# A decoder layer with routed experts: routing tile by tile, small fills of the output, first weights ahead of the lists, another first pair

## The chip, the cores and the metric

The kernel runs on one core of one Trainium2 chip. The metric is the device time of one execution in microseconds: the median over the runs, 5215.67 us for the kernel before (three runs, 5214.3 to 5219.2).

## The reference

2048 tokens of 1024 channels pass through one layer in float32:

```python
# token mix: three branches from one input projection, merged by sigmoid gates
z = h @ w_in                                  # conv B,C,h | gMLP u,v | attention q | gates
y_conv = cb * causal_depthwise_conv(cc * ch, conv_w)
y_gmlp = gmlp_spatial_gate(gelu(gu), gelu(gv), ...)
y_xa   = memory_cross_attention(q, mem_n, w_kv)
merged = g_conv*(y_conv@w_conv_proj) + g_gmlp*(y_gmlp@w_gmlp_proj) + g_xa*(y_xa@w_xa_proj)
x = layer_norm(ALPHA * x + merged @ w_out)
# experts: top 4 of 32, gate = softmax of the four logits
logits = x @ w_router + b_router
top_vals, top_idx = top_k(logits, 4)
g, u = split(xs @ w_gate_up[e] + b_gate_up[e], 2)       # xs: the tokens of expert e
act  = (clip(u, -7, 7) + 1) * (min(g, 7) * sigmoid(1.702 * min(g, 7)))
y[token] += gate * (act @ w_down[e] + b_down[e])
x = layer_norm(ALPHA * x + y)
```

## The kernel before

All large products run on TensorE as three passes of the fp32r type: each operand is split into a high part (ScalarE, line 75) and a low part (VectorE, line 76), and hi x hi, lo x hi and hi x lo are added in PSUM. A weight unit is 1 MB, [128 x 8 x 256]; SyncE loads it into a raw buffer (`load_unit`), the two engines split it by halves into a ring (`whi`, `wlo`). `run_items` walks one list of items (a weight source, a TensorE function, an epilogue): before each item it issues splits and loads some halves ahead. Work without weights stands as items with no source, or as functions in the list `bg`, of which one is taken per item. The engines run in the order in which this walk writes their instructions.

*Token mix.* Four chunks of 512 tokens. In chunk 1 sixteen items without weights (`fill`, line 807) write the last layer norm's bias over the output, 128 rows each, since final results are later added to it. In the last chunk the order is: projection unit 2 of the third branch (weights `vd`), output-weight units 0 and 1, projection unit 3, output-weight units 2 and 3, then four token tiles in which `last_pe` (line 1473) multiplies the merged gates with the output weights (PSUM `lo`), and `last_epi` (line 1499) adds the residual `r` and does the layer norm. `x1_tr` transposes the result for the router (`lg`). `route_tasks` (line 606) chooses the experts, places tokens in the `lists` by scatters on GpSimd, and forms the gates' transpose (`gT`) that starts the sum `yacc`. The first two tiles are routed together after the last `lo`, then the third and the fourth each.

*Experts.* `rank` (line 707) sorts the experts by load; each rank has a fixed capacity (`CAPS`: 552, 532, 476, 460, ... 260 for ranks 0, 1, 2, 3, 15; 216 down to 52 for ranks 16 to 31), and `number` reads the expert's id (`eid`) on SyncE. `ORDER` makes pairs of a light and a heavy rank; the first pair is the lightest and rank 15, and rank 2 is last. An expert has eight up units (g0, u0, ... u3) and four down units. SyncE loads its list (`lst`), GpSimd gathers tokens (`xg`), TensorE transposes them (`xsT`), the split gives `xs`. A heavy expert's ups have weights stationary and all tokens as columns (`up`), a light one's have tokens stationary (`tu`, token-major) and its activations are transposed (`acT`); downs are `dn`, scatter-added into `yacc`. The ups of one expert run between the downs of the one before. `bulk` (line 984) computes the last layer norm while the last expert's downs (`ld`, line 850) run, and `again` (line 1085) redoes the rows that the last expert changed.

The order of the first pair's parts, and the start before it:

```python
l, h, nxt = exps[:3]
l.number()
h.number()
def start(_):
    for x in (l, h):
        x.list()
...
(l,"g",0),(l,"u",0),(l,"g",1),(l,"u",1),(h,"g",0),(h,"u",0),(l,"g",2),(l,"u",2),
(h,"g",1),(h,"u",1),(l,"g",3),(l,"u",3), ...
```

Of the kernel before, what the change touches and what calls it, by code (L numbers as in the profile page):

```python
# [51 lines left out]


LAST = 2
FIRST = HALF - 1
# [6 lines left out]
class Kern:  # L62
    def __init__(self, ctx, tc, a, out, dbg=None):
        self.ctx, self.tc, self.nc, self.a, self.out, self.dbg = ctx, tc, tc.nc, a, out, dbg or {}
        self.items = []
        self.bg = []

        self.qt = []
        self.post = []
        self.scat = None  # L70
        self.loaded = False

# [33 lines left out]
    def item(self, src, pe, epi=None, split=None):  # L106
        self.items.append((src, pe, epi, split or self.split_half))


    def run_items(self, first=None):  # L110
# [7 lines left out]
        def load(upto):  # L118
            nonlocal nl
            while nl < min(upto, len(wi)):  # L120
                raws[wi[nl]] = self.load_unit(items[wi[nl]][0])
                nl += 1

# [15 lines left out]
        for i in range(n):  # L139
            if items[i][0] is not None:  # L140
                done += 1

                split(2 * done + self.whalves - 3)
                load(ns // 2 + self.wraws)
                split(2 * done + max(2, self.whalves - 2))
# [5 lines left out]
            if self.bg:  # L151
                self.bg.pop(0)()
            if items[i][2] is not None:
# [117 lines left out]
    def phase_a(self):  # L271
# [12 lines left out]
        with ExitStack() as c2:  # L284
# [3 lines left out]
            self.pm = c2.enter_context(tc.tile_pool(name="pm", bufs=1))  # L288
            self.pp = c2.enter_context(tc.tile_pool(name="pp", bufs=3, space=PSUM))
# [4 lines left out]
            self.bst = pa.tile([3 * NE, D], F32R, name="bst")  # L294
            self.gtt = pa.tile([3 * NE, TC], F32R, name="gtt")
# [18 lines left out]
            for c in chunks:  # L314
                c.emit(chunks[c.c + 1] if c.c + 1 < NCHUNK else None)
            self.run_items()
            while self.bg:
# [229 lines left out]
    def router(self, t, th, tl):  # L547
        nc = self.nc
        te, ve = nc.tensor, nc.vector
        ps = self.tr_psum("lg")  # L550
        for k in range(KT):
# [3 lines left out]
        sm = self.sm  # L555
# [50 lines left out]
    def route_tasks(self, c, ts, tag=("t4", 2)):  # L606
# [6 lines left out]
        def choose():  # L613
# [5 lines left out]
            scr = self.pa.tile([P, 2, TC], F32, tag=tag[0], name="rscr", bufs=tag[1])  # L619
            if n == 1:  # L620

                scr, S["scr"] = (scr[:, i, :].rearrange("p (a b) -> p a b", a=2) for i in range(2))
# [13 lines left out]
        def place():  # L636
# [5 lines left out]
            scr = S["scr"] if n == 1 else self.pa.tile([P, 2, TC], F32, tag="t4", name="rscr2", bufs=2)  # L642
# [14 lines left out]
            ent = sm.tile([P, n, TOPK, 2], I32, tag="ent", name="ent", bufs=2)  # L657
# [13 lines left out]

            for t in range(n):
# [9 lines left out]
        def spread():  # L682
            gs = S["gs"]
            pt = self.tr_psum("gT")
            for t in range(n):
                te.transpose(pt[: 3 * NE, t * P : t * P + P], gs[:, t].rearrange("p h e -> p (h e)"), self.ident)
            se.activation(self.gtt[:, t0 * P : (t0 + n) * P], pt[: 3 * NE, : n * P], AF.Copy)

        return [choose, place, spread]


    def yacc_init(self, c, t, r, hs=range(2)):
        nc = self.nc
        row = c * TC + t * P
        for q in hs:
# [4 lines left out]
            if c < NCHUNK - 1:  # L700
                nc.sync.dma_start(self.yacc[q][row : row + P, :], x)
        if c == NCHUNK - 1:
            for h in range(2):
                nc.scalar.dma_start(self.yacc[h][row : row + P, :], r[:, t, h * 512 : h * 512 + 512])
# [34 lines left out]
    def moe(self, c3):  # L739
# [5 lines left out]
        self.wp2 = c3.enter_context(tc.tile_pool(name="wp2", bufs=1))  # L745
        self.whalves, self.nhalf = 6, 0
# [4 lines left out]
    def experts(self):  # L751
# [4 lines left out]
        h.number()  # L756

        def start(_):
            for x in (l, h):
                x.list()  # L760
# [7 lines left out]
        def prep(t):  # L768
# [5 lines left out]
            (l, "g", 0), (l, "u", 0), (l, "g", 1), (l, "u", 1), (h, "g", 0), (h, "u", 0), (l, "g", 2), (l, "u", 2),  # L774
# [31 lines left out]
    def fill(self, t):  # L806
        self.nc.gpsimd.dma_start(self.out[t * P : t * P + P, :], self.a["ln2_b"][0].partition_broadcast(P))
# [133 lines left out]
    def block(self, i):  # L941
# [10 lines left out]
        y = self.px.tile([P, D], F32, tag="xsb", name="yg")  # L952
# [4 lines left out]
    def eitem(self, e, kind, j, todo=()):  # L957
# [19 lines left out]
        self.item((e, kind, j), pe, epi)  # L977
# [6 lines left out]
    def bulk(self):  # L984
# [4 lines left out]
        def load(i):  # L989
            for t in (2 * i, 2 * i + 1):  # L990
                y = S["y"][t % 6]
# [3 lines left out]
        def start():  # L995
# [5 lines left out]
            self.acc = [px.tile([P, D], F32, tag="xg", name="xa", bufs=2) for _ in range(2)] + [w[:, 1, :], S["y"][4]]  # L1001

            self.res = [px.tile([P, D], F32, tag="yrb", name="res"), S["y"][5]]
# [5 lines left out]
        def mean(i):  # L1009
            y1 = S["y"][(2 * i + 1) % 6]  # L1010
# [9 lines left out]
        def stats(i):  # L1020
            y0, y1 = (S["y"][t % 6] for t in (2 * i, 2 * i + 1))
# [27 lines left out]
        def apply(i):  # L1049
            rs, nmr = S.pop(i)  # L1050
            for n, t in enumerate((2 * i, 2 * i + 1)):
                y = S["y"][t % 6]
                se.activation(y, y, AF.Identity, scale=rs[:, n : n + 1], bias=nmr[:, n : n + 1])
                ve.tensor_tensor(y, y, self.g2, ALU.mult)  # L1054
            for t in (2 * i, 2 * i + 1):
                gp.dma_start(self.out[t * P : t * P + P, :], S["y"][t % 6], accum_op=ALU.add)  # L1056
# [11 lines left out]
        def second(i):  # L1068
# [25 lines left out]
    def redo(self, e, t, x, y):  # L1094
        gp, ve, sm = self.nc.gpsimd, self.nc.vector, self.sm
        m = e.rows(t)
        if e.r is None:
            self.bb2 = self.px.tile([P, D], F32, tag="X", name="bb2")
            self.bcast_row(self.bb2, self.a["ln2_b"][0])
            self.g2 = self.px.tile([P, D], F32, tag="acta", name="g2")  # L1100
# [15 lines left out]
class Chunk:  # L1116
# [12 lines left out]
    def emit(self, nxt):  # L1129
# [164 lines left out]
    def proj_item(self, b, w, src, j):  # L1294
# [4 lines left out]
        k.item(w[:, j * UC : j * UC + UC], pe, self.proj_epi(b, j))  # L1299

    def projections(self, b, w, src, js):
        for j in js:
            for i, item in enumerate((lambda: self.gate_item(b, j), lambda: self.proj_item(b, w, src, j))):
                item()
                if self.c == 1 and b < 2:
                    self.k.item(None, lambda _, t=(b * NU + j) * 2 + i: self.k.fill(t))
# [120 lines left out]
    def out_epi(self, j):  # L1427
        k, ve = self.k, self.k.nc.vector

        def epi(ps):  # L1430
            r = self.r[:, :, j * UC : j * UC + UC]
            ve.scalar_tensor_tensor(r, r, ALPHA, ps, ALU.mult, ALU.add)
            if j == NU - 1:
# [11 lines left out]
                choose, place, spread = k.route_tasks(self.c, range(TT))  # L1445
                k.bg += [lambda: (k.router_top(), choose()), lambda: None, place, spread]
# [26 lines left out]
    def last_pe(self, t):  # L1473
        k, te = self.k, self.k.nc.tensor

        def pe(_):
# [3 lines left out]
            for q in range(2):  # L1480
                for j in range(NU):

                    if t >= 2 and (q, j) == (0, 1):
                        k.router(t - 2, *self.x1t[t - 2])
                    if t >= 1 and (q, j) == (1, 2):
                        self.x1_tr(t - 1)
                    hi, lo = self.wo[j][q]
                    for kk in range(4):
                        kg = q * 4 + kk
                        first = kg == 0 and j % 2 == 0  # L1490
                        last = kg == KT - 1 and j % 2 == 1
                        o = ps[:, j, :]
                        te.matmul(o, xh[:, kg, tsl], hi[:, kk, :], start=first, stop=False)
                        te.matmul(o, xh[:, kg, tsl], lo[:, kk, :], start=False, stop=False)
                        te.matmul(o, xl[:, kg, tsl], hi[:, kk, :], start=False, stop=last)
# [436 lines left out]
```

## Time and profile before

| | |
|---|---|
| median of the runs | 5215.67 us |
| profiled execution | 5238.69 us, span 5237.0 us, mean granted clock 0.981 |
| TensorE matmul | 5065.8 us, 97% of the span |
| VectorE, ScalarE, GpSimd | 2886.8 (55%), 2034.9 (39%), 590.7 us (11%) |
| moved by DMA | 801.15 MB, mean 153 GB/s |

Times in the rows are us from the span's start. In a timeline a row is one run of equal instructions: start, length, engine, line, operation, output<-input, shape, count, and in brackets the idle time before it with what ended it. The clock is the TensorE clock that was granted, as a share of 2.4 GHz. In a table of windows, each engine's busy time stands with its count of instructions.

### The profile page before, as it was taken

Reading aid. Unit: us, or ns where it says so; the run is one execution under the profiler, and the core shown is the slowest. Engines: PE = TensorE matmul, PEld = TensorE weight load, DVE = VectorE, ACT = ScalarE, POOL = GpSimd, SP = SyncE. Lnnn points to the kernel's source line nnn. Section 1 sums busy time; section 2 is a strip of 40 time slices with the busy share of each in tenths; the row PEclk is TensorE's granted clock in tenths of the full one; section 3 lists DMA queues with packets and bytes.
Section 4 is the critical chain, followed back from the end, with each engine's and each line's share of the span. In section 5 each row is a group of like instructions: output and inputs, shape, how many; then the busy total and the mean of one; then the engine's idle time right before and its main releaser. Section 6 shows DMA issues by size and latency. Waiting matters only on the chain. (4 is left out here: it accounts for less than half of the span.)

```text
span 5237.0 us, 79154 instructions
## 1 busy us (share of the span) xinstructions
PE 5065.8 (97%) x32383; PEld 4642.8 (89%) x32383; DVE 2886.8 (55%) x4650; ACT 2034.9 (39%) x3023; POOL 590.7 (11%) x860
## 2 busy tenths in 40 slices
PE   9999999999999999999968999999999999999997
PEld 7888887788888878888758999999999999999996
DVE  5445345453545435443466555556666666666656
ACT  3333222232233332233234334444455555555543
POOL 0010001000010000100011012111111111111124
PEclk9999999999999999999978999999999999999998
DMA  5443333432332333322257456666766667766676
GB/s 169 153 154 106 103 109 110 134 123 97 113 113 89 105 112 108 103 89 89 97 163 225 152 147 189 185 184 194 208 202 199 189 204 210 209 199 201 201 224 159
DMA packets 764032, 801.15 MB, mean 153 GB/s; under 512 B 82992, under 2 KB 715912, under 8 KB 763664
## 3 DMA queue, kind: packets, MB, share of 16 engines
q1 hardware_dynamic: 704304, 665.58, 40.1%
q0 software_dynamic: 49760, 119.96, 9.3%
q10 hardware_dynamic: 9600, 10.49, 0.6%
q8 instruction: 257, 4.21, 0.3%
q14 instruction: 111, 0.91, 0.1%
HBM read 722.76 MB, written 81.54 MB: 154 GB/s over the span
## 5 line engine op out<-in xcount | busy, mean ns | idle before, releaser
L76 DVE TENSOR_TENSOR wlo<-raw,whi 128x1024 fp32r<-128x1024 f32 x1201 | 1429.3, 1222 | 1181.0 <-ACT whi L75 1167.6
L75 ACT ACTIVATE whi<-raw 128x1024 fp32r<-128x1024 f32 x1201 | 1218.2, 1049 | 704.3 <-PE mm L175 477.4
L1705 PE MATMUL up<-xs,whi 128*128 128x276 f32 (+16 forms) x2304 | 720.7, 313 | 5.4 <-ACT whi L75 2.1
L1707 PE MATMUL up<-xs,wlo 128*128 128x276 f32 (+16 forms) x2304 | 718.6, 312 | 2.3 <-DVE wlo L76 2.3
L174 PE MATMUL mm<-Xh,whi 128*128 128x512 f32 x1792 | 716.4, 400 | 2.8 <-ACT whi L75 2.8
L1706 PE MATMUL up<-xs,whi 128*128 128x276 f32 (+16 forms) x2304 | 718.2, 312 | 0.9 <-DVE xs L76 0.9
L176 PE MATMUL mm<-Xh,wlo 128*128 128x512 f32 x1792 | 710.9, 397 | 0.5 <-DVE wlo L76 0.4
L175 PE MATMUL mm<-Xl,whi 128*128 128x512 f32 x1792 | 707.9, 395 | 0.0
L1856 PE MATMUL dn<-whi,act 128*128 128x256 f32 (+5 forms) x1888 | 534.6, 283 | 0.6 <-ACT whi L75 0.6
L1857 PE MATMUL dn<-wlo,act 128*128 128x256 f32 (+5 forms) x1888 | 531.6, 282 | 1.8 <-DVE wlo L76 1.8
L1858 PE MATMUL dn<-whi,act 128*128 128x256 f32 (+5 forms) x1888 | 531.1, 281 | 0.0
L1705 PEld LDWEIGHTS up<-xs,whi 128*128 128x128 f32 x2304 | 436.3, 189 | 13.2 <-ACT whi L75 2.7
L1707 PEld LDWEIGHTS up<-xs,wlo 128*128 128x128 f32 x2304 | 436.2, 189 | 9.3 <-DVE wlo L76 2.9
L1706 PEld LDWEIGHTS up<-xs,whi 128*128 128x128 f32 x2304 | 436.3, 189 | 7.4 <-DVE xs L76 1.2
L1891 POOL DMA_INDIRECT yacc<-yr,lst x154 | 274.4, 1782 | 1426.4 <-ACT yr L1882 1410.0
L176 PEld LDWEIGHTS mm<-Xh,wlo 128*128 128x128 f32 x1792 | 336.9, 188 | 82.5 <-DVE wlo L76 1.6
L174 PEld LDWEIGHTS mm<-Xh,whi 128*128 128x128 f32 x1792 | 337.2, 188 | 79.6 <-ACT whi L75 3.2
L175 PEld LDWEIGHTS mm<-Xl,whi 128*128 128x128 f32 x1792 | 337.6, 188 | 78.1 <-issue 0.5
L1701 PE MATMUL up<-xs,whi 128*128 128x352 f32 (+7 forms) x1280 | 369.9, 361 | 0.0
L1857 PEld LDWEIGHTS dn<-wlo,act 128*128 128x128 f32 (+5 forms) x1888 | 347.6, 184 | 2.8 <-DVE wlo L76 2.5
L1856 PEld LDWEIGHTS dn<-whi,act 128*128 128x128 f32 (+5 forms) x1888 | 347.6, 184 | 2.0 <-ACT whi L75 1.1
L1858 PEld LDWEIGHTS dn<-whi,act 128*128 128x128 f32 (+5 forms) x1888 | 347.6, 184 | 0.0
(448 smaller groups left out, 9235.2 us busy)
## 6 DMA issues: line engine op xcount, KB each, us to landing
raw<-in_w_gate_up SPq DMA_DIRECT2D x256, 1024.0 KB
raw<-in_w_down SPq DMA_DIRECT2D x128, 1024.0 KB
raw<-in_w_in SPq DMA_DIRECT2D x127, 1024.0 KB
raw<-in_w_conv_proj SPq DMA_DIRECT2D x16, 1024.0 KB
raw<-md SPq DMA_DIRECT2D x16, 1024.0 KB
raw<-in_w_gmlp_proj SPq DMA_DIRECT2D x16, 1024.0 KB
raw<-vd SPq DMA_DIRECT2D x16, 1024.0 KB
raw<-in_w_out SPq DMA_DIRECT2D x16, 1024.0 KB
```

Of the source, the lines that this page charges most:

```text
L75: self.nc.scalar.activation(hi, src, AF.Copy)
L76: self.nc.vector.tensor_tensor(lo, src, hi.bitcast(F32), ALU.subtract)
L174: te.matmul(o, hi[:, k, cs], xh[:, kk, :], start=first, stop=False)
L175: te.matmul(o, hi[:, k, cs], xl[:, kk, :], start=False, stop=False)
L176: te.matmul(o, lo[:, k, cs], xh[:, kk, :], start=False, stop=last)
L1701: te.matmul(o, hi[:, kk, cs], xv, start=first, stop=False)
L1705: te.matmul(o, hi[:, kk, cs], xs[:, kg, 0, s0:s1], start=first, stop=False)
L1706: te.matmul(o, hi[:, kk, cs], xs[:, kg, 1, s0:s1], start=False, stop=False)
L1707: te.matmul(o, lo[:, kk, cs], xs[:, kg, 0, s0:s1], start=False, stop=last)
L1856: te.matmul(o, ah, hi[:, kk, :], start=first, stop=False)
L1857: te.matmul(o, ah, lo[:, kk, :], start=False, stop=False)
L1858: te.matmul(o, al, hi[:, kk, :], start=False, stop=last)
```

## The change

1. The output is filled by 128 transfers of 16 rows, in place of 16 of 128 rows; one is issued after each of the last 128 weight items of the token mix, and the items without weights are gone.
2. In the last chunk projection unit 3 stands ahead of the four output-weight units.
3. `last_pe` goes through the output weights in another order, and evicts the first half of a tile before its last twelve matmuls; transposes, router and routing follow tile by tile, and the gates of the third and fourth tile come after `rank`. One transpose block (`spread`) serves all tiles, and the start of `yacc` uses 1024 columns at once in the last chunk.
4. At the start of the experts only the light expert's id is read ahead of the first list; the second weight unit stands ahead of the biases.
5. Rank 3 (460 tokens) is in the first pair, ranks 4 to 15 move up, six light parts stand first, and the first four items split two halves fewer ahead.
6. Pools are moved (`pg`, `px2`), `bulk` uses eight row buffers in place of six, and the redo of rank 2's tiles goes as [2], [0, 1], [3] at its second, seventh and eighth step, where it was [0, 1, 2] and [3].

```diff
+FILL = 16
-FIRST = HALF - 1
+FIRST = 3
 HEAVY = [FIRST] + [r for r in range(HALF) if r not in (FIRST, LAST)] + [LAST]
...
-                split(2 * done + self.whalves - 3)
+                split(2 * done + self.whalves - 3 + min(items[i][4], 0))
                 load(ns // 2 + self.wraws)
-                split(2 * done + max(2, self.whalves - 2))
+                split(2 * done + max(2, self.whalves - 2) + items[i][4])
...
+            if self.gq and items[i][0] is not None:
+                self.gq.pop(0)()
...
+            late = sum(x[0] is not None for x in self.items) - SEQ // FILL
+            self.gq = [lambda: None] * late + [lambda t=t: self.fill(t) for t in range(SEQ // FILL)]
...
         l.number()
-        h.number()
         def start(_):
-            for x in (l, h):
-                x.list()
+            l.list()
+            h.number()
+            h.list()
+            self.load_ahead(2)
             l.gather(0)
             h.gather(0)
...
-            (l, "g", 0), (l, "u", 0), (l, "g", 1), (l, "u", 1), (h, "g", 0), (h, "u", 0), (l, "g", 2), (l, "u", 2),
+            (l, "g", 0), (l, "u", 0), (l, "g", 1), (l, "u", 1), (l, "g", 2), (l, "u", 2), (h, "g", 0), (h, "u", 0),
...
-            todo.setdefault(min(1 + t, 3), []).append(("after", lambda t=t: prep(t)))
+            todo.setdefault(min(1 + t, 4), []).append(("after", lambda t=t: prep(t)))
...
-            self.eitem(x, kind, j, todo.get(n, ()))
+            self.eitem(x, kind, j, todo.get(n, ()), -2 if n < 4 else 0)
...
-            self.wo_item(0)
-            self.wo_item(1)
-            self.proj_item(2, k.vd, "pr", NU - 1)
-            self.wo_item(2)
-            self.wo_item(3)
+            self.proj_item(2, k.vd, "pr", NU - 1, 2)
+            for j in range(NU):
+                self.wo_item(j)
...
-            for q in range(2):
-                for j in range(NU):
-                    if t >= 2 and (q, j) == (0, 1):
-                        k.router(t - 2, *self.x1t[t - 2])
-                    if t >= 1 and (q, j) == (1, 2):
-                        self.x1_tr(t - 1)
+            for i, (q, j) in enumerate(((0, 0), (0, 1), (1, 0), (1, 1), (0, 2), (1, 2), (0, 3), (1, 3))):
+                if i == 5 and t >= 1:
+                    if t >= 2:
+                        self.choose(t - 2)
+                    self.x1_tr(t - 1)
+                if i == 6 and t >= 2:
+                    self.rt[t - 2][1]()
+                    self.rt[t - 2][2]()
+                if i == 7:
+                    if t >= 1:
+                        self.lg[t - 1] = k.router(t - 1, *self.x1t[t - 1])
+                    self.evict(t, ps, 0)
...
-                third[0]()
-                self.x1_tr(t)
-                third[1]()
-                k.router(t, *self.x1t[t])
-                fourth[0]()
-                fourth[1]()
+                self.x1_tr(t, 0)
+                k.router_tile(t - 1, self.lg[t - 1])
+                self.x1_tr(t, 4)
+                self.choose(t - 1)
+                lg = k.router(t, *self.x1t[t], None, range(KT // 2))
+                self.rt[t - 1][1]()
+                k.router_tile(t, k.router(t, *self.x1t[t], lg, range(KT // 2, KT)))
+                self.choose(t)
+                self.rt[t][1]()
                 k.rank()
-                for f in (third[2], fourth[2]):
-                    f()
+                for i in (t - 1, t):
+                    self.rt[i][2]()
+                k.spread(*(self.rt[i][3] for i in range(TT)))
...
             if i == 0:
-                self.again(self.last, self.acc, range(3))
+                self.again(self.last, self.acc, [2])
             if i == NT // 2 - 2:
+                self.again(self.last, self.acc, [0, 1])
+            if i == NT // 2 - 1:
                 self.again(self.last, self.acc, [3])
```

GpSimd's queue of before around the end of chunk 1's scatters and the loads for the next chunk (`xm` and `r` are inputs, `out<-in_ln_b` a fill):

```order
L663 DMA lists<-ent,dst 131072x2
L807 DMA out<-in_ln_b 128x1024 x10
L335 DMA xm<-in_x 128x1024 x4
L807 DMA out<-in_ln_b 128x1024 x6
L1345 DMA r<-in_x 128x4x1024
L244 DMA lw<-in_ln_g 128x1024
L244 DMA lw<-in_ln_b 128x1024
```

and the same place after the change:

```order
L682 DMA lists<-ent,dst 131072x2
L841 DMA out<-in_ln_b 16x1024 x24
L348 DMA xm<-in_x 128x1024 x4
L841 DMA out<-in_ln_b 16x1024 x13
L1378 DMA r<-in_x 128x4x1024
L252 DMA lw<-in_ln_g 128x1024
L252 DMA lw<-in_ln_b 128x1024
L841 DMA out<-in_ln_b 16x1024 x15
L678 IOTA ent 128x16
```

The ten and six large fills became runs of small ones, of which others stand ahead of this place and behind the next chunk's scatters (7, 13, 15, 24, 13, 15, 37 and 4 in all).

SyncE's queue of before from the last chunk's weights to the first expert weights (`vd` third projection, `in_w_out` output weights, ids, lists, biases `bgu` and `bb`):

```order
L90 DMA raw<-vd 128x8x256
L90 DMA raw<-in_w_out 128x8x256 x2
L1534 DMA x1d<-r 128x1024 x4
L1596 TENSOR_LOAD eid
L1596 ISA x2
L1596 TENSOR_LOAD eid
L1596 ISA x2
...
L84 DMA raw<-in_w_gate_up 128x8x256
...
L1612 DMA bgu<-in_b_gate_up 128x16x1
...
L84 DMA raw<-in_w_gate_up 128x8x256
```

and after the change:

```order
L94 DMA raw<-vd 128x8x256 x2
L94 DMA raw<-in_w_out 128x8x256 x4
L1571 DMA x1d<-r 128x1024 x4
L1660 TENSOR_LOAD eid
L1660 ISA x2
...
L88 DMA raw<-in_w_gate_up 128x8x256
...
L1660 TENSOR_LOAD eid
...
L88 DMA raw<-in_w_gate_up 128x8x256
...
L1676 DMA bgu<-in_b_gate_up 128x16x1
```

The last projection unit moved ahead of the output weights; the second id is read behind the first list, and the second expert weight unit stands ahead of the biases where it stood behind them.

## Rows read from the trace of the kernel before

**Rows 1.** The page: busy us, share and instructions; moved GB/s in 40 slices.
```profile
PE 5065.8 (97%) x32383; PEld 4642.8 (89%) x32383; DVE 2886.8 (55%) x4650; ACT 2034.9 (39%) x3023; POOL 590.7 (11%) x860
GB/s 169 153 154 106 103 109 110 134 123 97 113 113 89 105 112 108 103 89 89 97 163 225 152 147 189 185 184 194 208 202 199 189 204 210 209 199 201 201 224 159
```

**Rows 2.** Windows: length; busy (count) of PE, PEld, DVE, ACT, POOL; clock, DMA share, GB/s.
```profile
2549.30:2571.30 22.00, 13.85 (x50) 10.33 (x49) 11.15 (x12) 7.17 (x8) 0.00 (x0) 0.77 0.30 96
2627.70:2675.20 47.50, 18.20 (x71) 13.15 (x70) 31.27 (x118) 4.95 (x14) 20.88 (x37) 0.53 0.33 100
2675.20:2705.70 30.50, 17.06 (x91) 15.29 (x91) 19.39 (x27) 15.22 (x22) 0.91 (x1) 0.67 0.82 266
2705.70:2788.20 82.50, 71.29 (x527) 68.40 (x527) 56.97 (x95) 36.87 (x57) 2.67 (x4) 0.92 0.63 199
2715.57:2721.30 5.73, 5.73 (x50) 5.73 (x49) 3.46 (x6) 2.79 (x4) 0.00 (x0) 1.00 0.28 91
2788.20:2861.00 72.80, 60.81 (x432) 57.66 (x432) 55.34 (x85) 38.25 (x58) 14.90 (x14) 0.85 0.80 248
4061.00:4191.00 130.00, 130.00 (x991) 129.54 (x990) 84.16 (x143) 66.88 (x115) 24.70 (x27) 1.00 0.67 195
5085.00:5145.00 60.00, 60.00 (x281) 52.24 (x279) 37.62 (x58) 31.84 (x42) 32.25 (x90) 1.00 0.76 205
```

**Rows 3.** Timeline of PE around the last projection unit.
```profile
2549.27 0.40 PE L176 MATMUL mm<-Bh,wlo 128*128 128x512 f32 x1
2557.40 0.79 PE L174 MATMUL mm<-Bh,whi 128*128 128x512 f32 x1 [7.73 <-ACT whi L75]
```

**Rows 4.** Timeline of DVE from the first eviction to the ids.
```profile
2587.37 1.22 DVE L1508 SCALAR_TENSOR_TENSOR r<-r,lo 128x1024 f32<-128x1024 f32 x1 [7.72 <-PE lo L1495]
...
2626.34 0.16 DVE L615 TENSOR_TENSOR gt<-v 128x8 f32<-128x8 f32 x1
...
2633.01 1.22 DVE L1508 SCALAR_TENSOR_TENSOR r<-r,lo 128x1024 f32<-128x1024 f32 x1
...
2648.39 0.14 DVE L615 TENSOR_TENSOR gt<-v 128x4 f32<-128x4 f32 x1
...
2654.00 0.19 DVE L680 TENSOR_TENSOR rscr<-rscr 128x32 f32<-128x32 f32 x1
...
2657.26 0.18 DVE L734 CAST eid<-eid 1x32 int32<-1x32 f32 x1 [0.47 <-PE eid L732]
```

**Rows 5.** Timeline of POOL: r load, last scatter, first gather.
```profile
2577.61 0.80 POOL L1345 DMA_DIRECT2D r<-in_x  x1 [419.51 <-DVE Al L76]
...
2657.46 0.96 POOL L663 DMA_INDIRECT lists<-ent,dst  x1 [0.19 <-issue]
2667.71 0.96 POOL L1669 DMA_INDIRECT xg<-x1d,lst  x1 [9.29 <-DMA lst<-lists]
```

**Rows 6.** Timeline of SP's queue: first and second weight unit.
```profile
2659.36 0.41 SPq L84 DMA_DIRECT2D raw<-in_w_gate_up  x1
...
2670.23 19.02 SPq L84 DMA_DIRECT2D raw<-in_w_gate_up  x5
```

**Rows 7.** Timeline of PE in the first parts of pair 1.
```profile
2675.18 0.58 PE L1727 MATMUL tu<-whi,xs 128*128 128x256 f32 x1 [1.38 <-ACT whi L75]
...
2683.54 0.58 PE L1727 MATMUL tu<-whi,xs 128*128 128x256 f32 x1 [3.53 <-ACT whi L75]
...
2705.69 0.58 PE L1705 MATMUL up<-xs,whi 128*128 128x260 f32 x1 [1.86 <-ACT xs L75]
```

**Rows 8.** Timeline of POOL: fills in chunk 1.
```profile
904.60 4.18 POOL L807 DMA_DIRECT2D out<-in_ln_b  x8
909.75 0.52 POOL L807 DMA_DIRECT2D out<-in_ln_b  x1 [0.96 <-DMA out<-in_ln_b]
```

**Rows 9.** Timeline of PE, chunk 1, some 65 us behind the fills.
```profile
977.03 0.50 PE L174 MATMUL mm<-Ah,whi 128*128 128x512 f32 x1 [3.65 <-ACT whi L75]
```

**Rows 10.** Timeline of POOL at the end: the redo's last gathers.
```profile
5178.59 1.29 POOL L1089 DMA_INDIRECT yyy<-yacc,lst  x1 [5.76 <-DMA out<-yyy]
```

More of the change, by code (lines that the diff above doesn't have):

```diff
@@ L104, in split_half, with item @@
         return hi, lo
[L106 to L107 removed]
+    def item(self, src, pe, epi=None, split=None, ahead=0):
+        self.items.append((src, pe, epi, split or self.split_half, ahead))
     def run_items(self, first=None):
@@ L618, in choose @@
             ve.tensor_copy(idf, self.i8[:, sl, :TOPK])
-            scr = self.pa.tile([P, 2, TC], F32, tag=tag[0], name="rscr", bufs=tag[1])
-            if n == 1:
-                scr, S["scr"] = (scr[:, i, :].rearrange("p (a b) -> p a b", a=2) for i in range(2))
+            if room is not None:
+                scr, S["scr"] = (room[:, i * 256 : i * 256 + 256].rearrange("p (a b) -> p a b", a=2) for i in range(2))
+            else:
+                scr = self.pa.tile([P, 2, TC], F32, tag="t4", name="rscr", bufs=2)
             eq = S["eq"] = scr[:, 0, : n * P].rearrange("p (t k e) -> p t k e", t=n, k=TOPK)
@@ L694, in yacc_init @@
         row = c * TC + t * P
+        if c == NCHUNK - 1:
+            ps = self.pp.tile([P, 2, 512], F32, tag="mm", name="gb")
+            for h in hs:
+                nc.tensor.matmul(ps[:, h, :], self.gtt[:, t * P : t * P + P], self.bst[:, h * 512 : h * 512 + 512], start=True, stop=True)
+            x = r[:, t, :]
+            nc.vector.scalar_tensor_tensor(x, x, ALPHA, ps.rearrange("p h c -> p (h c)"), ALU.mult, ALU.add)
+            for h in hs:
+                nc.scalar.dma_start(self.yacc[h][row : row + P, :], x[:, h * 512 : h * 512 + 512])
+            return
         for q in hs:
@@ L699, in yacc_init @@
             nc.vector.scalar_tensor_tensor(x, x, ALPHA, ps, ALU.mult, ALU.add)
[L700 to L704, printed above, removed]
+            nc.sync.dma_start(self.yacc[q][row : row + P, :], x)
     def rank(self):
@@ L1298, in pe @@
             return k.mm_ch(wt, *getattr(self, src), TC)
-        k.item(w[:, j * UC : j * UC + UC], pe, self.proj_epi(b, j))
+        k.item(w[:, j * UC : j * UC + UC], pe, self.proj_epi(b, j), ahead=ahead)
     def projections(self, b, w, src, js):
         for j in js:
[L1303 to L1306, printed above, removed]
+            self.gate_item(b, j)
+            self.proj_item(b, w, src, j)
     def gate_epi(self, b, j):
@@ L1496, in pe @@
-            return ps
-        return pe
+            if t == 0:
+                self.lg, self.rt = {}, {}
+            for i, (q, j) in enumerate(((0, 0), (0, 1), (1, 0), (1, 1), (0, 2), (1, 2), (0, 3), (1, 3))):
[10 more added lines that the diff above has]
+                    self.evict(t, ps, 0)
+                hi, lo = self.wo[j][q]
+                for kk in range(4):
+                    kg = q * 4 + kk
+                    first = kg == 0 and j % 2 == 0
+                    last = kg == KT - 1 and j % 2 == 1
+                    o = ps[:, j, :]
+                    te.matmul(o, xh[:, kg, tsl], hi[:, kk, :], start=first, stop=False)
+                    te.matmul(o, xh[:, kg, tsl], lo[:, kk, :], start=False, stop=False)
+                    te.matmul(o, xl[:, kg, tsl], hi[:, kk, :], start=False, stop=last)
```

125 lines of the change are left out of this document (72 added, 53 removed).

## The prediction

> **What bounds the kernel now.** I read the page first. TensorE is busy 97% of the span [rows 1], so only work that leaves TensorE, or holes and half-clock stretches in its stream, can move the time. The table of windows then shows where the rest lies. A full expert pair (4061 to 4191) has 991 matmuls without a gap at clock 1.00, with VectorE busy 84 of 130 us and the DMA engines at 0.67. The passage from the token-mix part to the experts is different: from 2549.3 to 2861 TensorE is busy for parts of it only and at clocks from 0.53 to 0.92 [rows 2]. I price each of its windows by full-rate work. 48 up matmuls of 260 columns take 5.73 us at clock 1.00 [rows 2], 0.119 us each, and I take that for 256 columns too:
> - 2549.3 to 2571.3: 48 matmuls of 512 columns, 0.238 each, are 11.4 of 22.0 us, 10.6 lost.
> - 2627.7 to 2675.2 (routing, lists, first gather): 71 matmuls, most of them small; nearly all of the 47.5 us is latency.
> - 2675.2 to 2705.7 (first light parts): 91 matmuls, 10.9 us, 19.6 lost.
> - 2705.7 to 2788.2 (the rest of pair 1): 512 x 0.119 = 61 and some 2 for 15 transposes, so 63 of 82.5, 19.5 lost.
> - 2788.2 to 2861 (the downs of pair 1's heavy expert beside the light expert of pair 2): 432 x 0.119 = 51.4 of 72.8, 21.4 lost.
>
> The timelines name what ended the waits: a weight half split on ScalarE at 2557.40 [rows 3], the routing chain on VectorE that ends with the expert ids at 2657.26 [rows 4], the last scatter and the gather on GpSimd [rows 5], the first weight transfers on SyncE at 2659.36 and 2670.23 [rows 6], and again weight halves at 2683.54 [rows 7].
>
> **The change, part by part.**
>
> *The last projection unit before the output weights (10.6 lost above).* TensorE ends the unit before at 2549.6 and waits 7.73 us [rows 3], for a half that ScalarE splits behind two output-weight halves. With that unit next in every queue its load goes out two ring places sooner and its half is split first. I let it end at 2560.7, 10.6 sooner. The r load on GpSimd waits for VectorE's last split of the merged gates and goes out at 2577.61 [rows 5]; it moves with them, so the first eviction (2587.37, which waited 7.72 us for TensorE [rows 4]) comes at 2576.8.
>
> *Routing by tile.* From that eviction to the expert ids VectorE takes 70.1 us, 24.4 of them after the last tile's eviction at 2633.01 [rows 4]. Routing each tile by itself costs VectorE more: the two tiles that were routed together took 6.7 us (2626.3 to 2633.0), the fourth alone 5.8 (2648.4 to 2654.2) [rows 4], so the four take 23.2 in place of 18.3, 5 us more. What it takes away are waits beside it, and 2.2 us of gate work that now stands behind the ids. I put a tile at 18.6 us (layer norm 6.1, choice, place, gates and logits 6.7, splits 2.6, eviction 1.4, waits 1.8), so the last eviction is at 2576.8 + 3 x 18.6 = 2632.6 and the ids 20 us later, at about 2652, 5 sooner. Bounds: all 14 us of VectorE's waits in this stretch gone, -16; the added work all on the path, +2.
>
> *Lists and first weights.* The first raw unit stood ahead of the lists before, and still does; new are one register load fewer ahead of it and the second unit ahead of the bias loads, where it went out at 2670.23, 10.9 us after the first [rows 6]. The gather waited 9.29 us for its list [rows 5], and the first light part began 7.5 us after the gather [rows 7]. With the ids 5 sooner, about 1 from the register load and 2 from the state writes that now start later, the first part begins at 2667: **-8** (0 to -16).
>
> *Six light parts first, rank 3 in place of rank 15.* Later pairs lose 200 tokens of heavy expert, pair 1 gains them. The price: 281 matmuls of 476 columns take 60.0 us [rows 2], 0.2135 each, so 0.206 at 460 columns and 9.9 us for a part of 48, against 5.73. Eight parts: +33.5. The downs go from 64 to 96 matmuls of 256 columns each, four times 32 x 0.119: +15.2. Together 48.7 us leave pairs that run gapless [rows 2], so those lose **48.7**, and as much enters a stretch with 60 us of loss. What VectorE, ScalarE and the DMA engines do there grows little: the count of weight units is the same.
> - First light parts: two more of them (3.8 us) fill time in which the heavy tiles were prepared; 30.5 becomes 31.5: **+1** (0 to +4). The first four parts split two halves fewer ahead, so that ScalarE and VectorE reach the gathered tiles sooner; if that starves a part, it waits as at 2683.54, 3.5 us [rows 7], which is the upper end.
> - Rest of pair 1: 63 + 33.5 - 3.8 = 92.7 us of work. Losses between zero and the 19.5 of before: 92.7 to 112. VectorE has 57 us of work there and the DMA engines 0.63 of 82.5 = 52 [rows 2], so neither fills 93, and a part that lasts 9.9 covers the split of its successor's halves where one of 5.7 did not. I take 6 of loss, 98.7: **+16.2**.
> - Downs beside pair 2's light expert: 51.4 + 15.2 = 66.6, up to 88 with the old loss. VectorE's 55 plus about 4 for the fourth tile and the DMA engines' 58 [rows 2] lie below. Again 6 of loss, 72.6: **-0.2**.
>
> Sum of the passage: -8 + 1 + 16.2 - 0.2 - 48.7 = -39.7; with no loss behind the first light parts -52, with all of the old loss -11.
>
> *Small fills.* Eight fills of 512 KB went out at 904.60 without a pause and the next waited on one of them [rows 8]; the same stretch ends in a TensorE wait of 3.65 us for a half, with half clock behind it [rows 9], some 5 to 6 us. In after 128 fills of 64 KB stand in GpSimd's order in runs of at most 37, and one issue is 0.52 us [rows 8]; with eight in flight a run of 37 moves 2.4 MB in 19 us or more, 125 GB/s at most, beside the 89 to 134 of those chunks [rows 1], together under the 266 that the passage moved [rows 2]. GpSimd's 128 x 0.52 = 67 us lie beside idle time: behind the 37 stands the last chunk's r load, for which GpSimd idled 419 us [rows 5], behind the last four the next scatters, tens of us later. The bias loads, now behind the second unit, are needed only at a part's end, and chunk 1's loop loses its sixteen empty items. **-5** (-8 to +11).
>
> The Trainium skill's page "DMA: Bandwidth & Descriptors" (section Bandwidth, Measured) speaks against this: batch to 1 MiB, since small transfers are ruled by their descriptors; its table has 0.95 us for 64 KB and 6.15 for 1 MB. By it, an estimate, the 8 MB of fills would hold the DMA engines for 122 us in place of 49, and weights behind them would come late. Whether they do is a rival below, priced from rows.
>
> *End of the program.* Redoing rank 2's early tiles was split 3 + 1, the last waiting 5.76 us for a buffer [rows 10]; now 1 + 2 + 1 with eight row buffers. That wait was hidden behind the last downs for the most part; the end is set by the last additions and scatters, which stay. **-2** (-8 to +5).
>
> Total: -39.7 - 5 - 2 = -46.7. The profiled execution took 5238.7 us, 23 above the median of the runs shown; its sum gives 5192, and against the median of 5215.67 it gives **5169 us**.
>
> **Rivals.**
> 1. *The first pair is bound by its preparation.* Four tiles must be gathered, transposed and split in place of three, VectorE still splits a half in each part, and the losses stay at 19.5 and 21.4. For it: TensorE's waits in this stretch are for splits on ScalarE and VectorE [rows 7]. Against: those engines have room [rows 2]. Then the passage gives -11 and the total is -18: 5198.
> 2. *The fills collide in every chunk.* One stall like that at 977 in chunks 1, 2 and 3: 3 x 5.7 in place of 5.7, +11 in place of -5. For it: 61 of the fills follow directly on two blocks of scatters. Against: the eight-in-flight limit above. Total -39.7 + 11 - 2 = -31: 5185. This is where the skill's rule would show.
> 3. *Slower: the low clock lasts through the heavy parts.* The clock granted before them is 0.53 and then 0.67, near 1.2 GHz where TensorE had idled [rows 2]. Each heavy part at that level costs 9.9 more than at 2.4, and there are eight: +79 - 47 = +32, 5248. It decides from five parts on (5 x 9.9 = 49). For it: 260-column parts too began low at 2705.69, after a wait [rows 7]. Against: ten us later a whole part ran at 1.00 [rows 2].
> 4. *The swap doesn't pay.* The pairs that get lighter run against the DMA engines or VectorE and don't shorten by 48.7: no change, 5216. Against: 0.67 and 84 of 130 in a full pair [rows 2]. The first weights, too, were ahead of the lists already.
>
> **Numbers.** The forecast has 0.60 (its own range, from its bounds of loss and ids, 5156 to 5186), rival 1 0.17, rival 2 0.10, rival 3 0.06, rival 4 0.07. A measurement of this kernel tells 0.2%, about 10 us, from no change. So faster 0.87 (forecast, rivals 1 and 2), same 0.07, slower 0.06. The range reaches to rival 1 above and near the passage without loss below: 5148 to 5203.
>
> **What would show it.** Expert ids and first light part 5 and 8 us sooner; the windows from first heavy part to pair 2's first heavy up longer by some 15 us in sum but with TensorE busy over 92%; a later pair, as the fifteenth, with its matmuls gapless and the sum of the later pairs 48 us shorter; no wait for in_w_in weights after the scatters of chunks 1 to 3. I am wrong if heavy parts of pair 1 show waits before each half (rival 1), if ScalarE waits on raw loads beside runs of fills (2), or if the granted clock stays near 0.5 past the second heavy part (3).

## The result, and the profile after

The changed kernel takes 5155.91 us (median of four runs, 5155.29 to 5156.73), the kernel before 5214.99 beside it: a ratio of 0.9886, interval 0.9869 to 0.9904, or 59 us less. The forecast was 5169 us, 47 less, with 5148 to 5203 as its range.

The page of the changed kernel; its columns are those of [rows 1]:

```profile
span 5154.0 us, 79275 instructions
PE 5033.1 (98%) x32385; PEld 4621.1 (90%) x32385; DVE 2890.2 (56%) x4675; ACT 2034.1 (39%) x3023; POOL 650.2 (13%) x973
```

Profile against profile the spans differ by 83 us, not 59, because the profiled execution of before was 23 us above its median. A second profile of the kernel before (experiment e1) has a span of 5209.7 us, and every comparison of stages below is with that one where nothing else is said. The difference stands in chunks 1 to 3: from chunk 0's router stage to the first eviction the first profile takes 24.6 us more (1740.0 against 1715.4). The windows of the changed kernel that answer to [rows 2] (columns as there): routing up to the ids, ids to first light part, first light parts, from the first heavy part to pair 2's first heavy part in two pieces and whole, a full pair, and the end.

```profile
2536.90:2608.00 71.10, 52.96 (x408) 51.47 (x409) 54.61 (x191) 7.03 (x15) 14.99 (x30) 0.81 0.12 44
2608.00:2628.70 20.70, 6.27 (x20) 3.76 (x20) 7.45 (x16) 2.70 (x7) 4.42 (x7) 0.50 0.82 257
2628.70:2663.30 34.60, 24.45 (x133) 22.79 (x134) 27.74 (x42) 19.95 (x28) 5.71 (x4) 0.70 0.86 272
2663.30:2764.00 100.70, 97.24 (x509) 87.38 (x508) 61.10 (x82) 37.77 (x49) 2.69 (x4) 0.98 0.51 164
2764.00:2834.00 70.00, 66.86 (x544) 65.07 (x544) 48.70 (x70) 36.36 (x56) 17.64 (x16) 0.98 0.82 241
2663.30:2834.00 170.70, 164.11 (x1053) 152.46 (x1052) 109.80 (x151) 74.13 (x104) 20.34 (x20) 0.98 0.63 196
4038.00:4168.00 130.00, 130.00 (x999) 129.55 (x998) 90.52 (x159) 70.14 (x124) 24.89 (x27) 1.00 0.72 210
5069.60:5154.00 84.40, 52.19 (x385) 50.42 (x384) 52.96 (x96) 22.86 (x27) 39.30 (x92) 0.78 0.54 130
```

The same stages in the second profile of the kernel before:

```profile
2562.80:2632.50 69.70, 51.25 (x396) 49.87 (x395) 51.55 (x170) 7.46 (x16) 16.81 (x32) 0.81 0.10 36
2632.50:2651.80 19.30, 7.17 (x18) 3.42 (x18) 6.28 (x12) 2.20 (x6) 4.22 (x6) 0.50 0.85 251
2651.80:2679.20 27.40, 16.80 (x90) 14.74 (x90) 19.38 (x27) 15.23 (x22) 1.60 (x1) 0.71 0.85 274
2679.20:2833.40 154.20, 130.36 (x959) 124.69 (x959) 112.27 (x179) 75.15 (x114) 17.66 (x18) 0.91 0.72 223
5116.00:5209.70 93.70, 53.65 (x384) 51.16 (x384) 56.46 (x102) 24.75 (x30) 37.06 (x93) 0.75 0.56 137
```

From the first heavy part on, TensorE was idle for 23.8 of 154.2 us at a clock of 0.91; now it is idle for 6.6 of 170.7 at 0.98. All stages together, forecast beside measured (from the first start of each stage in the two profiles):

| stage | forecast | measured |
|---|---|---|
| chunks 1 and 2, to the last chunk's router stage | -5 | -13.5 |
| from there to the first eviction | -10.6 | -12.1 |
| first eviction to the ids | +5.6 | +1.4 |
| ids to first light part | -3 | +1.4 |
| first light part to first heavy part | +1 | +7.1 |
| to pair 2's first heavy part | +16 | +16.6 |
| later pairs, to the last expert's downs | -48.7 | -47.0 |
| last downs to the end | -2 | -9.3 |
| sum | -46.7 | -55.4 |

### The profile page after: what moved, and what is told of

It is laid out like the page before. It is cut to its first block, busy times and chain, and to the rows that moved or that the text cites. A ratio compares the mean times of both kernels' runs of the same rounds, so it can differ in the third digit from the quotient of the medians.

```text
span 5154.0 us, 79275 instructions
## 1 busy us (share of the span) xinstructions
PE 5033.1 (98%) x32385; PEld 4621.1 (90%) x32385; DVE 2890.2 (56%) x4675; ACT 2034.1 (39%) x3023; POOL 650.2 (13%) x973
```

## The experiments

Twelve kernels were run. They fall into three groups, each on another chip. The first two, e1 to e4 and e5 to e8, stand beside runs of before with medians of 5213.9 and 5213.6, and are set against the 5155.9 of the changed kernel. The last four stand beside runs of before with a median of 5241.65, and the changed kernel was not run beside them, so these are compared by stages. Each variant has one profile, and one stage varies between kernels whose code there is the same: from the first eviction to the ids the changed kernel takes 71.1 us, and e3, e7 and e8 70.8 to 71.1, at a granted clock of 0.81 to 0.84; the other seven variants of it take 73.4 to 73.9 at 0.78 or 0.79. In that stage a difference of 3 us between two profiles shows nothing by itself.

**e1: the kernel before, once more.** No edit.

> The kernel before, unchanged, for a second profile and a measure of the noise. The profiled execution of before took 23 us more than the median, and three stretches of about 10 us in chunks 1 to 3 (896 to 907, 1527 to 1537, 2149 to 2160) show the transposing matmuls at 0.72 us each with idle time put down to issue; the profile after has none of them. Theory A: they belong to that one execution; this profile has none, its span is about 5214, and the change in chunks 2 and 3 is near nothing. Theory B: they belong to the kernel; this profile shows them again at about the same places, 7 us lost each, and part of the change's gain is that they are gone. Time against before: 1.000 within 0.002 either way.

Measured: 5212.31 us, ratio 0.9995 (0.9985 to 1.0004); span 5209.7. Theory A holds for this profile: none of the three stretches is there. In chunk 1 TensorE waits for halves in three places, and behind the second and third of them the granted clock is 0.50 for 3.4 us each:

```profile
941.37 0.50 PE L174 MATMUL mm<-Ah,whi 128*128 128x512 f32 x1 [2.27 <-ACT whi L75]
...
956.64 0.50 PE L174 MATMUL mm<-Xh,whi 128*128 128x512 f32 x1 [3.00 <-ACT whi L75]
...
973.21 0.50 PE L174 MATMUL mm<-Ah,whi 128*128 128x512 f32 x1 [2.79 <-ACT whi L75]
```

The change shortens chunk 1's stage by 14.0 us against this profile (625.8 to 611.8); these waits, the shorter ones for low parts just behind them (2.0 us in all) and half of the 6.8 us at half clock come to 13.4.

But "one execution only" was too narrow: the stretches are in the profiles of all four kernels of the last group too (whose times are 28 us longer for the kernel before), as here in e9:

```profile
896.63 0.28 PE L203 MATMUL mt<-wlo,Xh 128*128 128x256 f32 x1 [0.53 <-issue]
...
897.36 0.28 PE L202 MATMUL mt<-whi,Xh 128*128 128x256 f32 x1 [0.32 <-issue]
...
908.29 0.80 PE L730 MATMUL gb<-bst,gtt 96*128 96x512 f32 x1 [4.07 <-DVE r L732]
```

They come with old and new code alike: the first profile of before has them too. Whether they go with the chip was not tried, nor what makes them.

**e2: the old first pair in the changed kernel.**

```diff
-FIRST = 3
+FIRST = HALF - 1
...
-    (l,"g",2), (l,"u",2), (h,"g",0), (h,"u",0),
+    (h,"g",0), (h,"u",0), (l,"g",2), (l,"u",2),
...
-            todo.setdefault(min(1 + t, 4), ...
+            todo.setdefault(min(1 + t, 3), ...
...
-    ... -2 if n < 4 else 0)
```

> The changed kernel with the old first pair alone undone (rank 15 with the lightest, four light parts first, the old places of the tiles' preparation, no smaller lookahead). Theory: the swap gives 25 to 35 us of the 59, since 48.7 us of heavy work leave gapless pairs and the first pair takes them into its lost time; expected 5181 to 5191. Rival: the first pair is bound by its preparation and the gain comes from the earlier lists and the token mix; then 5156 to 5168.

Measured: 5180.34 us, 24.4 more. The later pairs are 48.1 us longer, the stretch from the ids to pair 2 is 26.1 shorter (226.0 to 199.9). So the swap, with the order of parts that goes with it, is worth 24 us by the runs and 22.0 by these two stages (2.6 more stand in the stage that varies): just under the low end of the theory and far from the rival.

**e3: sixteen large fills at the old place.**

```diff
-FILL = 16
+FILL = 128
...
+            self.gq = []
...
+                if self.c == 1 and b < 2:
+                    self.k.item(None, lambda _, t=(b * NU + j) * 2 + i: self.k.fill(t))
```

> The changed kernel with sixteen fills of 128 rows as items without weights in chunk 1, as before. Theory: the wait of 3.65 us for a weight half at 977 and the half clock behind it come back, +5 to +8, 5161 to 5164. Rival: the fills cost nothing and chunk 1 gained by something else: 5154 to 5158.

Measured: 5173.37 us, 17.5 more, of which 16.6 stand in chunk 1's stage (628.4 against 611.8). The direction is the theory's, the size is not. The three waits are back, in sum longer than the single one of [rows 9]:

```profile
942.08 0.51 PE L182 MATMUL mm<-Ah,whi 128*128 128x512 f32 x1 [2.80 <-ACT whi L79]
...
957.35 0.50 PE L182 MATMUL mm<-Xh,whi 128*128 128x512 f32 x1 [1.46 <-ACT whi L79]
...
973.92 0.49 PE L182 MATMUL mm<-Ah,whi 128*128 128x512 f32 x1 [4.12 <-ACT whi L79]
```

**e4: the swap alone in the kernel before.**

```diff
-FIRST = HALF - 1
+FIRST = 3
```

> The kernel before with rank 3 in place of rank 15 in the first pair, and nothing else. Theory: two thirds of the lost time of pair 1 and the light stage behind it are filled without the six light parts too: -48.7 + 33.5 + 15.2 of work and 28 less loss, so -24 to -32, 5183 to 5191. Rival (preparation-bound): four tiles must be ready before the heavy parts and the losses stay: -10 to 0, 5205 to 5215.

Measured: 5196.17 us, ratio 0.9965 (0.9951 to 0.9979): 17.7 less than before, between the theory and the rival. Later pairs -45.7, ids to pair 2 +31.3 (200.9 to 232.2).

**e5: the last projection unit back in its old place.**

```diff
-            self.proj_item(2, k.vd, "pr", NU - 1, 2)
-            for j in range(NU):
-                self.wo_item(j)
+            self.wo_item(0)
+            self.wo_item(1)
+            self.proj_item(2, k.vd, "pr", NU - 1)
+            self.wo_item(2)
+            self.wo_item(3)
```

> The changed kernel with the last projection unit back between the second and the third output-weight unit. Theory (the first tile's end moves with that unit, and the routing chain with it): the first eviction comes 10 to 12 us later and the whole time too, 5166 to 5168. Rival (VectorE's chain of layer norms and routing sets the ids, whatever TensorE does before): 0 to +4, 5156 to 5160.

Measured: 5172.02 us (5166.35 to 5174.15), 16 more, above the theory's 5166 to 5168 and far from the rival. The old wait is there again, and the first eviction 11.3 us later; VectorE waits for the r load in both kernels, and GpSimd sends that load when VectorE has split the last of the merged gates (`Al`):

```profile
2519.44 0.79 PE L182 MATMUL mm<-Bh,whi 128*128 128x512 f32 x1 [7.72 <-ACT whi L79]
...
2539.57 0.80 POOL L1380 DMA_DIRECT2D r<-in_x  x1 [381.69 <-DVE Al L80]
...
2548.17 0.69 DVE L1554 SCALAR_TENSOR_TENSOR r<-r,lo 128x512 f32<-128x512 f32 x1 [6.56 <-DMA r<-in_x]
```

The changed kernel:

```profile
2528.30 0.80 POOL L1378 DMA_DIRECT2D r<-in_x  x1 [375.43 <-DVE Al L80]
...
2536.91 0.69 DVE L1552 SCALAR_TENSOR_TENSOR r<-r,lo 128x512 f32<-128x512 f32 x1 [4.30 <-DMA r<-in_x]
```

The load lands 8.5 us after its issue in both, and the eviction follows at once. So the unit's 11.3 us pass on whole, by way of the gates' split and the r load, and what is late next is that load, 4.3 us. At the ids the difference is 14.1; the further 2.8 stand in the stage that varies.

**e6: the old start of the experts.**

```diff
         l.number()
+        h.number()
...
             l.list()
-            h.number()
             h.list()
-            self.load_ahead(2)
```

> The changed kernel with the start of the experts as before: both ids read ahead of the first list, the second weight unit behind the biases. The first light part begins 20.7 us after the ids in the changed kernel and 19.3 in the kernel before. Theory: this part of the change gains nothing, 5153 to 5158. Rival (the forecast's -3 for it is hidden by another loss): the first light part 3 us later and 5159 to 5161.

Measured: 5160.37 us (5156.00 to 5164.25), ratio 0.9897 (0.9881 to 0.9912), which is the rival's number by its median, but can't be told from the changed kernel's: its lowest run lies among that kernel's. The first light part comes 18.8 us after the ids, 1.9 sooner than in the changed kernel, and pair 2 227.6 after them, 1.6 later. No gain of 3 is to be seen at the first part, so the stages go the theory's way; the ids themselves come 2.4 us later, in the stage that varies. Whether the start is worth a few us later stays open.

**e7: four light parts first, rank 3 kept.**

```diff
-    (l,"g",2), (l,"u",2), (h,"g",0), (h,"u",0),
+    (h,"g",0), (h,"u",0), (l,"g",2), (l,"u",2),
...
-            todo.setdefault(min(1 + t, 4), ...
+            todo.setdefault(min(1 + t, 3), ...
...
-    ... -2 if n < 4 else 0)
```

> The changed kernel with four light parts first, the old places of the tiles' preparation and the old lookahead, rank 3 kept. Swapping the rank alone in the kernel before gave 232 us from the ids to pair 2's first heavy part, the changed kernel has 226. Theory: the six parts are worth these 6 us, 5160 to 5164. Rival: the six parts only postpone the heavy tiles, which are ready no sooner; 5153 to 5158.

Measured: 5164.40 us, 8.5 more; ids to pair 2 232.8 in place of 226.0. That is the theory's 6 us, and with e4 it accounts for the swap alone having gained 18.

**e8: the old order of the redo, eight buffers kept.** In this kernel the redo writes to row buffers that still hold other rows, so those final rows are not the layer's result.

```diff
-                self.again(self.last, self.acc, [2])
+                self.again(self.last, self.acc, range(3))
...
-                self.again(self.last, self.acc, [0, 1])
-            if i == NT // 2 - 1:
```

> The changed kernel with the redo of rank 2's tiles in the old order, [0, 1, 2] at the second step and [3] at the seventh, the eight row buffers kept. The last downs take 84 us to the end where the kernel before took 94; in a profile of before ScalarE waits 7.08 us for a row buffer's load with the activations of the last expert behind it. Theory A (the eight buffers gain it): 5153 to 5159. Theory B (the order of the redo gains it): 5162 to 5166.

Measured: 5162.34 us, 6.4 more. That is theory B's number, but the stages speak against B: from the last downs to the end it takes 87.2 us, as other variants of the changed kernel do (84.4 to 87.1), and 4.1 of the 6.4 stand in the stage before, where the three redos now run. Since the buffers clash here, the order by itself is not settled by it.

**e9: the old end of the program.** Six row buffers and their two for the redo.

```diff
-                y = S["y"][t % 8]
+                y = S["y"][t % 6]
...
-            S["y"] += [px.tile([P, D], F32, tag="xg", name="yx", bufs=2) for _ in range(2)]
...
-            self.acc = S["y"][:2] + [w[:, 1, :], S["y"][2]]
+            self.acc = [px.tile([P, D], F32, tag="xg", name="xa", bufs=2) for _ in range(2)] + [w[:, 1, :], S["y"][4]]
...
-                self.again(self.last, self.acc, [2])
+                self.again(self.last, self.acc, range(3))
...
-                self.again(self.last, self.acc, [0, 1])
-            if i == NT // 2 - 1:
```

> The changed kernel with the end of the kernel before: six row buffers, redo [0, 1, 2] and [3] with their own two buffers, the overflow's gather where it was. Theory: this part is worth the 5 to 9 us by which the last downs to the end got shorter (93.7, 94.8 before and with the swap alone; 84 to 87 in the variants of the changed kernel), since ScalarE waits for a row buffer's load in front of the last expert's splits; 5161 to 5165. Rival: those us are where the program happens to stand; 5154 to 5158.

Measured: 5201.65 us, ratio 0.9923 (0.9909 to 0.9936), in the last group. The last downs to the end take 92.5 us; the other three kernels of that group have 84.3 to 86.9. So the new end, buffers and order together, is worth 5.6 to 8.1 us, as the theory has it. In the second profile of before, ScalarE shows how (timeline; the last downs' activations stand behind the wait) and TensorE what it costs:

```profile
5135.48 1.06 ACT L1015 ACTIVATE junk<-gby 128x1024 bf16<-128x1024 f32 x1 [7.08 <-DMA gby<-yacc]
5136.53 0.58 ACT L75 ACTIVATE act<-ut 128x476 fp32r<-128x476 f32 x1
...
5137.17 0.58 PE L850 MATMUL ld<-whi,act 128*128 128x256 f32 x1 [4.53 <-ACT act L75]
```

e9 has the same two waits, longer:

```profile
5128.73 1.06 ACT L1048 ACTIVATE junk<-gby 128x1024 bf16<-128x1024 f32 x1 [9.01 <-DMA gby<-yacc]
...
5130.42 0.58 PE L884 MATMUL ld<-whi,act 128*128 128x256 f32 x1 [6.15 <-ACT act L79]
```

In the changed kernel the wait of 4.53 is 1.45:

```profile
5085.16 0.39 PE L884 MATMUL ld<-whi,act 128*128 128x256 f32 x1 [1.45 <-ACT act L79]
```

**e3b and e3c: size and place of the fills apart.**

```diff
+# e3b: 128 rows each, one per eight of the last 128 weight items
+FILL = 128
...
+            self.gq = [lambda: None] * late + [(lambda t=t: self.fill(t // 8)) if t % 8 == 0 else (lambda: None) for t in range(128)]
...
+# e3c: 16 rows each, eight in every empty item of chunk 1
+            self.gq = []
...
+                        for n in range(8):
+                            self.k.fill(8 * t + n)
```

> The changed kernel with sixteen fills of 128 rows at the new places (one where every eighth small one stood, over the last 128 weight items, no empty items). With e3 (large fills at the old place, 17 us slower) and e3c it tells size from place. Theory (eight large writes in flight take the DMA engines from the weights; GpSimd still reaches several of these in a row): waits for weight halves again behind the scatters, 5159 to 5170. Rival (the place and the empty items were the trouble): 5154 to 5158.

> The changed kernel with 128 fills of 16 rows at the old place, eight in each of the sixteen empty items of chunk 1. Theory (size decides, since eight small ones in flight hold little of the DMA engines): 5154 to 5160. Rival (place decides, 8 MB at once in chunk 1 is too much in any size): 5165 to 5175, and waits for weight halves at 940 to 975 as with the large ones.

Measured: 5191.98 (0.9906, 0.9891 to 0.9921) and 5197.31 us (0.9918, 0.9904 to 0.9931). The intervals overlap; the stage tells more. It runs from chunk 0's router stage to chunk 1's. In this group that is 628.9 us for small fills at the old place, 624.0 for large ones at the new places, and 621.2 and 623.0 for the two kernels with small fills there; the first profile of before, which has the same stretches, has 630.1. e3c shows why small size did not help: GpSimd sends 17 without a pause and goes on until 957, and TensorE waits as before at 975:

```profile
904.94 8.27 POOL L841 DMA_DIRECT2D out<-in_ln_b  x17
...
975.11 0.80 PE L182 MATMUL mm<-Ah,whi 128*128 128x512 f32 x1 [3.63 <-ACT whi L79]
```

So in this group the place decides (6 to 8 us), the size 1 to 3 at most, while two kernels with the same fills differ by 1.8: e3c went the rival's way, and e3b lies between. How the 16.6 us of e3 divide on the other chips was not measured. Of the place itself, the sixteen empty items and the 8 MB at once were not taken apart.

**x_first1: rank 1 in the first pair.**

```diff
-FIRST = 3
+FIRST = 1
```

> The changed kernel with rank 1 (532 tokens, five tiles) in the first pair in place of rank 3 (460), as a version that might beat both. Theory: between the first heavy part and pair 2 only some 6 us of waits are left, and a fifth tile has to be prepared; the further work moved there, about 19 us, finds nothing to fill: 5152 to 5164. Rival (the gain goes on with the tokens moved, 24 us for 200): 9 us less, 5147.

Measured: 5191.93 us, 0.9908 (0.9892 to 0.9923). Against the changed kernel's profile, ids to pair 2 is 26.8 us longer (252.8) and the later pairs 23.3 shorter: nothing gained, as the theory has it. None of the versions tried shows itself faster than the changed kernel, the last four by their stages alone.

## Why the prediction was right, point by point

*The swap, the largest term.* Right in mechanism and size. The later pairs lost 47.0 us (48.7 forecast), and the heavy stretch of pair 1 grew by 16.6 (16): the work went into the lost time. What TensorE still waits for there is 6.4 us in six waits, the two longest of them

```profile
2709.53 0.48 PE L1768 MATMUL up<-xs,whi 128*128 128x460 f32 x1 [1.81 <-ACT whi L79]
...
2764.74 0.39 PE L1790 MATMUL tu<-whi,xs 128*128 128x256 f32 x1 [1.81 <-ACT whi L79]
```

where I took 6 and 6 of loss. Counted as I counted it, as time beyond 159.3 us of full-rate work, the loss is 11.4 of 12: the 6.6 idle, and 4.8 in which the work ran below that rate. Rival 1 (bound by preparation) falls with this, rival 4 with the later pairs, rival 3 with the clock of 0.98.

*First light parts, +1 (0 to +4).* Mis-sized: +7.1, beyond its bounds. I let the work of two more parts, 3.8 us at full clock, lie in idle time. But TensorE's idle time stayed what it was (10.2 of 34.6 us, before 10.6 of 27.4) and its busy time grew by 7.7, at a mean granted clock of 0.70, 0.50 in three pieces of the stretch. The waits did not shrink: the fourth tile, too, had to be gathered, transposed and split ahead of the heavy parts, and brought waits of its own:

```profile
2637.81 1.62 POOL L1732 DMA_INDIRECT xg<-x1d,lst  x1 [5.82 <-DMA xg<-x1d,lst]
...
2645.39 1.15 POOL L1732 DMA_INDIRECT xg<-x1d,lst  x1 [5.97 <-PE xsT L1743]
...
2659.18 0.77 PE L1743 MATMUL xsT<-ident,xg 76*128 76x76 f32 x4 [3.92 <-DVE act L80]
```

The gathers have two buffers; the last waits for the transposes of an earlier tile, and lands 9.2 us after its issue, just ahead of its own first transposes (2654.78). The second half of these waits 3.92 us more for VectorE, which splits the light expert's activations only behind four low parts of weight halves:

```profile
2654.33 4.62 DVE L80 TENSOR_TENSOR wlo<-raw,whi 128x1024 fp32r<-128x1024 f32 x4
2658.87 0.25 DVE L80 TENSOR_TENSOR act<-acT,act 128x104 fp32r<-128x104 f32 x1
```

That is rival 1's mechanism (tiles to prepare while VectorE splits weights), at work ahead of the heavy parts and not in them.

*Ids and lists, -8 together with the projection unit.* Measured -9.3 up to the first light part (-12.1 + 1.4 + 1.4), from other shares. The projection unit passed on in full (e5), though by the r load and not by TensorE's end, from which I had the eviction start. VectorE's chain grew by 1.4, not 5.6, in this profile; in the seven with the lower clock there it grew by 3.7 to 4.2. The last step failed: I put the first part 3 us sooner after the ids. One reason is argued and not shown: with routing finished before the gates, the ids (2608.03) are ahead of the last scatter (2609.88), where [rows 4, 5] have them together, and the lists can only be read after it:

```profile
2609.88 0.96 POOL L682 DMA_INDIRECT lists<-ent,dst  x1 [0.19 <-issue]
...
2614.69 1.75 SPq L1666 DMA_DIRECT2D lst<-lists  x2
...
2619.54 0.96 POOL L1732 DMA_INDIRECT xg<-x1d,lst  x1 [8.70 <-DMA yacc<-r]
```

Against it as the whole reason: in e6 the last scatter is as late behind the ids (1.86 us), and the first part comes 18.8 after them. Over the kernels with the new start that time runs from 19.5 to 21.7, so the +1.4 itself is within what one profile leaves open; the missing 3 us are not.

*Fills, -5.* Mis-sized: -13.5 by stages, 17.5 by e3. I priced one stall [rows 9], from a profile that shows one where e1 shows three. And the ground was too narrow: I put it on eight large fills in flight, but e3c's small ones at the old place cost nearly as much (628.9 against 630.1), so the place counts more. The rule of the Trainium skill's page "DMA: Bandwidth & Descriptors" (section Bandwidth, Measured) that small transfers cost more did not decide the time here: 128 fills of 64 KB at the new places show no wait for a weight load in chunks 1 to 3, and cost no more than 16 of 512 KB (e3b). Nor did they hold the DMA engines longer: of GpSimd's queue the pages of e1 and of the changed kernel show packets, MB and the share of the 16 engines' span that the packets took:

```profile
q0 software_dynamic: 49760, 119.96, 9.6%
q0 software_dynamic: 51552, 119.96, 9.4%
```

Rival 2 falls.

*The end, -2.* Mis-sized: -9.3. I followed GpSimd's wait for a buffer [rows 10] and held it to be hidden, and did not look at ScalarE, whose wait for the same buffers stood ahead of the last expert's splits (e9). In the profile that I had, this wait was small, though: 2.19 us on ScalarE and 1.56 on TensorE, with 90.3 us from the last downs to the end, where e1 has 7.08, 4.53 and 93.7. Against that profile the end gained 6.0, and e9 puts it at 5.6 to 8.1.

The total came out 12 us short by the runs and 9 by the stages: three terms were taken too small (fills 8.5, end 7.3, the chain to the ids 5.7), two too favourably (lists 4.4, first parts 6.1), and the later pairs with the heavy stretch by 2.3. So the total owes its nearness in part to luck: errors of 21.5 us one way and 12.8 the other. The measured time lies at the lower edge of the forecast's own range, 5156 to 5186, and well inside the stated one.

## What to carry to other kernels

Work that must be done anyway can fill a stretch in which the busiest engine waits for something else; price it by the rate that the engine has in that stretch (full in the heavy parts, half in much of the light ones), and stop where its waits there are used up (here 6 of 171 us). Before a profile is summed up, compare its own time with the runs: 23 us above the median meant that one of its features, here a set of issue gaps, is not in the runs that are compared. For every buffer that is waited for, look at all engines that wait for it, and at what stands behind each of them in its queue.

## What was not expected of the hardware

The kernel before took 5213 to 5215 us in some groups of runs and 5241.65 in another, on another chip, where each profile had stretches at the start of chunks 1 to 3 in which the product matmuls (`mt`) start some 0.7 us apart, where 0.12 is usual. With them the stages of chunks 1 to 3 took 9 to 12 us longer each, with the same code there (e9 and x_first1 against the changed kernel). The new fills were worth less there (6 to 8 us of chunk 1's stage) than elsewhere (14 to 17).
